# Which engine issues a scan's stores, how often its norm's factors are stored, and where its state is scaled

## The chip, the cores and the metric

The kernel runs on one core of one Trainium2 chip. It uses TensorE (PE in the profile), VectorE (DVE), ScalarE (ACT), GpSimd (POOL), and SyncE (SP), which here issues DMAs and does nothing else. The metric is the time of one execution on the device in microseconds. A time on the chip is the median of a few runs; beside it stands one profiled execution, whose trace every duration below is from.

## The reference

One layer of a decoder: 1024 rows of width 1024, all in f32. A causal block mixes a gated short convolution (A) with a Mamba-2 scan (S) and ends with a gated MLP. Cut to what matters here:

```python
u = rmsnorm(h)
gate_a, gate_s, b_a, c_a, v_a, z, xbc, dt = split(u @ w_in)
A = (b_a * causal_dwconv3(c_a * v_a)) @ w_a_out
xs, B, C = split(silu(causal_dwconv4(xbc) + bias))
# scan: 4 groups of 8 heads of 64, state 128, in chunks of 128 rows
seg = a_cum[l] - a_cum[s]                       # per head, masked causally
y_diag = ((C @ B.T) * exp(seg)) @ (x * dt)
states = B.T @ (x * dt * exp(a_cum[-1] - a_cum))
state  = state * exp(a_cum[-1]) + states        # from chunk to chunk
y = y_diag + (C @ state_before) * exp(a_cum) + d_skip * x
y = y * silu(z)
S = (y * rsqrt(mean(y * y over the group's 512) + eps) * w_norm) @ w_s_out
h = h + (sigmoid(gate_a) * A + sigmoid(gate_s) * S) @ w_o
v = rmsnorm(h)
h = h + (silu(causal_dwconv3(v @ w_1) + b) * (v @ w_3)) @ w_down
out = rmsnorm(h)
```

## The kernel before, in words

**Products.** Activations lie transposed: 128 features on the partitions, rows along the free axis. An f32 product is made of rounded halves: `split` (L148, L149) casts an operand on ScalarE to a high part and takes the rest on VectorE or GpSimd, and `product` (L255) makes 12 matmuls of 128x512 (high by high, high by low, low by high, over four blocks). Two column blocks of a projection are one `Pair`: seven such products on sums and differences of operands and weights (names b11, b21, t1, t2, t3, t4, b22). `load` (L158) brings the weights into three buffers `raw`; seven products use two loads. So while a `Pair` runs, TensorE needs a cast of ScalarE every twelve matmuls, and the names of its waits carry the `Pair`: pt1z is the product with t1 of a pair of z, pt4xb that with t4 of a pair of xBC, pb22cv that with b22 of a pair of c_a and v_a.

**The projections.** First come the gates of group A (`head`), then the list BEFORE and the list BESIDE: xBC (`xbc_pair`, with a convolution of four taps and a Silu in `conv4`), z (`z_pair`, Silu), c_a with v_a (`ca_pair`), b_a (`ba_pair`) and the gates (`gate_pair`, Tanh in `gates_done`). Their results go to DRAM: xBC and z of group g to `xd_[g]`, with ten slots of 128 features for each group (four of x, one of B, one of C, four of z; L545 and L561), b_a's product to `tad` (L586), the gates to `gad` and `gsd` (L596). Before, SyncE issues all of these stores, with those of c_a's branch.

**The scan.** 32 chunks s = 8 g + c (group g of 4, chunk c of 8; a name such as m2_1 is m of group 2, chunk 1) run beside the list BESIDE. `ssd_chunk` is a generator cut into eight parts. A counter `tick` goes up with every product of a `Pair`; chunk s has its due time at 12 + 6 s, and its parts come at fixed distances from it (L53, L54): m's load at -11, the load of `in` at -8, the decay at -6, the transposes at -4, the load of z at -3, the chunk's products at 0, the squares at +3, the norm's factor at +6.

The parts of a chunk, in order:

1. m (L630): the running sums of the decay, one row for each head, from `acd`, sent to all 128 partitions, 128x1024; two buffers.
2. `in` (L633): six slots of `xd_`, 128x6x128; two buffers.
3. The decay, on ScalarE: eight Relu with a bias (L639, one for each head), then one Exp over m (L640).
4. x and B transposed (px L645, pb), C by B (pc L649), x by dt (xd L651, VectorE), x by the decay to the chunk's end (xe L658, eight on ScalarE), d_skip by x (L662, GpSimd), the copy bk of B's transpose (L666, ScalarE, one buffer), C by B masked (L668) and times m (L669).
5. eb (L675), the exp of the running sums, by two loads from `ead`; zt (L680), the four slots of z, one buffer.
6. pd (L687), eight matmuls with m; po (L694), C by the state; pst (L700), B by x. Then y's sum and the state:

```python
        dve.tensor_tensor(xt, xt, tiles(pd), op=ALU.add)          # L701
            dve.tensor_tensor(eb, po, eb, op=ALU.mult)            # L703
            pool.tensor_tensor(xt, xt, tiles(eb), op=ALU.add)     # L704
                pool.tensor_tensor(heads(st), heads(st), ...)     # L711
                dve.tensor_tensor(st, st, pst, op=ALU.add)        # L715
        dve.tensor_tensor(xt, xt, zt, op=ALU.mult)                # L717
        sp.dma_start(yd[g, c // 4][:, :, hts], xt)                # L718
```

7. Squares of y (L721, ScalarE, into eb), two sums on VectorE (L722, L724).
8. pn (L727), a matmul with ones that sums over the partitions; the mean and eps (L729); the power -0.5 (L731, GpSimd) into r, one column of 128 values; r's store into `rd` (L732), half a kilobyte.

x and y stand in the tile of `in` (xt is its first four slots), which is why its rows in the profile are called `in`. y goes to `yd[g, half]`, and y's factors to `rd[g, half]`, each half being four chunks. Both are read again later by `y_half`, for the product with w_s_out.

**After the list** the last chunks run out beside nothing (the loop at L762), and the program goes on with the gated sum of A (`ta_half`, `y_a`), S (`y_half`, `s_out`), w_o, and the MLP. `w_sums` (L779 loads w_down, L770 subtracts, L787 stores the sums to `td`) is given to s_out and y_a as work beside them; its operations need nothing of the mixer.

**What sets the order.** The code is written in the order of the parts, but a scheduler, with a timeline simulation of its own, puts each instruction in its engine's list; each engine then works its list in order. So `w_sums` stands among the last chunks. An instruction that waits holds all that is behind it on its engine, DMA issues included. A DMA takes one of eight completion semaphores in turn over SyncE and ScalarE, and before it issues it waits until the DMA that had the semaphore before has landed. The buffers are rings: m's load of chunk s waits until pd of chunk s - 2 has read m; `in` of chunk s waits until y's store of chunk s - 2 has landed and its squares are done.

The functions touched are `conv4`, `z_pair`, `gates_done` and `ssd_chunk`; `tiny` (L131) gives the small columns.

Of the kernel before, what the change touches and what calls it, by code (L numbers as in the profile page):

```python
# [11 lines left out]
ALU = mybir.AluOpType  # L12
# [3 lines left out]
P = 128  # L16
# [6 lines left out]
HG = NH // NG  # L23
HD = 64
# [3 lines left out]
NCH = SEQ // P  # L28
# [37 lines left out]
def tile_block(  # L66
# [25 lines left out]
    pe, dve, act, pool, sp = nc.tensor, nc.vector, nc.scalar, nc.gpsimd, nc.sync  # L92
# [14 lines left out]
    def big_tile(name, dt=F32, shape=(P, 4, HALF)):  # L107
        return big.tile(list(shape), dt, tag="big", name=name, bufs=NBIG)
# [4 lines left out]
    def b4(name, shape=(P, SEQ)):  # L113
        return cur["b4"].tile(list(shape), F32, tag="b4", name=name, bufs=cur["n"])
# [16 lines left out]
    def tiny(name, w=1):  # L131
        return scr.tile([P, w], F32, tag="tiny", name=name, bufs=12)
# [7 lines left out]
    def const(shape, name, src=None):  # L140
        t = cst.tile(shape, F32, name=name)
        if src is not None:
            sp.dma_start(t, src)
        return t
# [18 lines left out]
    nhalf = const([P, 1], "nhalf")  # L163
# [167 lines left out]
    xd_ = [dram.tile([P, 10, SEQ], F32, name=f"ssd_in{g}") for g in range(NG)]  # L331
# [5 lines left out]
    yd, rd = {}, {}  # L337
# [20 lines left out]
    for t in range(0, NCH, 2):  # L358
        xt = big_tile(f"x{t}", shape=(P, 2, DM))
# [17 lines left out]
    cdb = scm.tile([P, 4, NH, 2], F32, name="cdb")  # L377
# [51 lines left out]
    for j in range(0, 4, 2):  # L429
# [3 lines left out]
        p = Pair(U, w_in[GA + j], w_in[GA + j + 1], f"g{GA + j}", cur["row"])  # L433
        p.first(b4(f"gt{j}"), True)
        head.append(p)
    p = Pair(U, w_in[GA + 4], w_in[GA + 5], f"g{GA + 4}")
# [88 lines left out]
    def ssd_slot(t):  # L525

        return (t // 4, t % 4) if t < 16 else ((t - 16) % 4, 4 + (t - 16) // 4)

    def taps(cv, ci, w, b):

        n = w.shape[1]
        act.activation(  # L532
            cv, ci[:, n - 1 : n - 1 + SEQ], AF.Identity, scale=w[:, n - 1 : n], bias=b
        )
        for j in range(n - 1):
            dve.scalar_tensor_tensor(  # L536
                cv, ci[:, j : j + SEQ], w[:, j : j + 1], cv, op0=ALU.mult, op1=ALU.add
            )

    def conv4(ci, t):  # L540
        cv = b4(f"cv{t}")
        taps(cv, ci, scw[:, t, :], scb[:, t : t + 1])
        act.activation(cv, cv, AF.Silu)
        g, slot = ssd_slot(t)
        sp.dma_start(xd_[g][:, slot, :], cv)  # L545

    def xbc_pair(t):
        cis = [s4(f"xbc{t + i}") for i in range(2)]
# [7 lines left out]
    def z_pair(t):  # L556
        zs = [b4(f"z{t + i}") for i in range(2)]
        pair(U, w_in[ZZ + t], w_in[ZZ + t + 1], f"z{t}", *zs)
        for i, z in enumerate(zs):
            act.activation(z, z, AF.Silu)  # L560
            sp.dma_start(xd_[(t + i) // 4][:, 6 + (t + i) % 4, :], z)  # L561


    taken = {}
# [28 lines left out]
    def gates_done(gts, dst, j):  # L593
        for i, gt in enumerate(gts):
            act.activation(gt, gt, AF.Tanh, scale=0.5)
            sp.dma_start(dst[:, j + i, :], gt)  # L596

    for i, p in enumerate(head):
        if i:
# [9 lines left out]
    def heads(t):  # L609
        return t.rearrange("p (h d) -> p h d", h=HG)  # L610

    def tiles(t):
        return t.rearrange("p (j l) -> p j l", j=4)

    states, stats = {}, {}

    def ssd_chunk(s):

        g, c = divmod(s, NCH)
        nm = f"{g}_{c}"  # L620
        q, cc = c // 2, c % 2
        hsl = slice(g * HG, (g + 1) * HG)
        ts = slice(c * P, (c + 1) * P)
        hts = slice((c % 4) * P, (c % 4 + 1) * P)

        hq = slice(q * NH + g * HG, q * NH + (g + 1) * HG)


        m = ssp.tile([P, HG, P], F32, tag="m", name=f"m{nm}", bufs=2)
        sp.dma_start(m, acd[cc, hq].unsqueeze(0).to_broadcast([P, HG, P]))  # L630
        yield
        inp = ssp.tile([P, 6, P], F32, tag="in", name=f"in{nm}", bufs=2)
        sp.dma_start(inp, xd_[g][:, 0:6, ts])  # L633
        xt, bt, ct = inp[:, 0:4, :], inp[:, 4, :], inp[:, 5, :]
        yield

        for h in range(HG):
            a = tk[:, 0, cc, q, g * HG + h : g * HG + h + 1]
            act.activation(m[:, h, :], m[:, h, :], AF.Relu, bias=a)  # L639
        act.activation(m, m, AF.Exp, scale=-1.0)  # L640
        yield

        px = sd_tile(f"px{nm}")
        for j in range(4):
            pe.transpose(px[:, j * P : (j + 1) * P], xt[:, j, :], ident)  # L645
        pb = sd_tile(f"pb{nm}")[:, :P]
        pe.transpose(pb, bt, ident)
        pc = sd_tile(f"pc{nm}")[:, :P]
        pe.matmul(pc, bt, ct, start=True, stop=True)  # L649
        xd = c2(f"xd{nm}")  # L650
        dve.tensor_tensor(  # L651
            heads(xd), heads(px),
            tk[:, 1, cc, q, hsl].unsqueeze(2).to_broadcast([P, HG, HD]), op=ALU.mult,
        )
        xe = c2(f"xe{nm}")
        for h in range(HG):
            hc = slice(h * HD, (h + 1) * HD)
            act.activation(  # L658
                xe[:, hc], px[:, hc], AF.Copy,
                scale=tk[:, 2, cc, q, g * HG + h : g * HG + h + 1],  # L660
            )
        pool.tensor_tensor(  # L662
            xt, xt, dsk[:, 4 * g : 4 * g + 4].unsqueeze(2).to_broadcast([P, 4, P]), op=ALU.mult,
        )
        bk = ssp.tile([P, P], F32, tag="bk", name=f"bk{nm}", bufs=1)
        act.copy(bk, pb)  # L666
        cb = ssp.tile([P, P], F32, tag="cb", name=f"cb{nm}", bufs=1)
        dve.tensor_tensor(cb, pc, tri, op=ALU.mult)  # L668
        dve.tensor_tensor(m, m, cb.unsqueeze(1).to_broadcast([P, HG, P]), op=ALU.mult)  # L669
        yield  # L670

        eb = c2(f"eb{nm}")
        if c > 0:
            for i in range(2):
                sp.dma_start(  # L675
                    tiles(eb)[i * HD : (i + 1) * HD],
                    ead[cc, hq.start + i : hq.stop : 2].unsqueeze(0).to_broadcast([HD, 4, P]),
                )
        zt = ssp.tile([P, 4, P], F32, tag="z", name=f"zt{nm}", bufs=1)
        sp.dma_start(zt, xd_[g][:, 6:10, ts])  # L680
        yield

        st = states.get(g)
        pd = sd_tile(f"pd{nm}")
        for h in range(HG):
            i, j = h % 2, h // 2
            pe.matmul(  # L687
                pd[i * HD : (i + 1) * HD, j * P : (j + 1) * P],
                xd[:, h * HD : (h + 1) * HD], m[:, h, :], start=True, stop=True,
            )  # L690
        if st is not None:
            po = sd_tile(f"po{nm}")
            for j in range(4):
                pe.matmul(  # L694
                    po[:, j * P : (j + 1) * P], st[:, j * P : (j + 1) * P], ct,
                    start=True, stop=True,
                )
        if c < NCH - 1:
            pst = sd_tile(f"pst{nm}")
            pe.matmul(pst, bk, xe, start=True, stop=True)  # L700
        dve.tensor_tensor(xt, xt, tiles(pd), op=ALU.add)  # L701
        if st is not None:
            dve.tensor_tensor(eb, po, eb, op=ALU.mult)  # L703
            pool.tensor_tensor(xt, xt, tiles(eb), op=ALU.add)  # L704
        if c < NCH - 1:
            if st is None:
                st = ssp.tile([P, HALF], F32, tag="st", name=f"st{g}", bufs=1)
                act.copy(st, pst)
                states[g] = st
            else:  # L710
                pool.tensor_tensor(  # L711
                    heads(st), heads(st),
                    cdb[:, q, hsl, cc : cc + 1].to_broadcast([P, HG, HD]), op=ALU.mult,
                )
                dve.tensor_tensor(st, st, pst, op=ALU.add)  # L715

        dve.tensor_tensor(xt, xt, zt, op=ALU.mult)  # L717
        sp.dma_start(yd[g, c // 4][:, :, hts], xt)  # L718
        yield
        sq = eb  # L720
        act.activation(sq, xt.rearrange("p j l -> p (j l)"), AF.Square)  # L721
        dve.tensor_tensor(sq[:, : 2 * P], sq[:, : 2 * P], sq[:, 2 * P :], op=ALU.add)  # L722
        sums = ssp.tile([P, P], F32, tag="ss", name=f"ss{nm}", bufs=1)
        dve.tensor_tensor(sums, sq[:, :P], sq[:, P : 2 * P], op=ALU.add)  # L724
        yield
        pn = sd_tile(f"pn{nm}")[:, :1]
        pe.matmul(pn, sums, ones[:, :1], start=True, stop=True)  # L727
        rs = tiny(f"yss{nm}")
        dve.tensor_scalar(rs, pn, 1.0 / HALF, EPS, op0=ALU.mult, op1=ALU.add)  # L729
        r = tiny(f"yr{nm}")  # L730
        pool.tensor_tensor(r, rs, nhalf, op=ALU.pow)  # L731
        sp.dma_start(rd[g, c // 4][hts].unsqueeze(1), r)  # L732
        yield

    def at(n, f):
# [261 lines left out]
    for i in range(NFF):  # L997
# [5 lines left out]
        cv = b4(f"fcv{i}")  # L1003
# [221 lines left out]
```

## Time and profile before

| what | value |
|---|---|
| median of 3 runs | 2109.27 us (2107.75 to 2114.36) |
| the profiled execution | 2107.57 us |
| its span in the trace | 2105.9 us |
| mean granted clock of TensorE | 0.967 of full speed |
| DMA, mean over the span | 161 GB/s |

The page's slices (40 of 52.6 us each) show where the engines are full. Each digit is a busy share in tenths, the last row the granted clock:

```profile
PE   6899998997998989897899999997999999999998
DVE  8756986755676557664567562438776677784555
ACT  5354455444744553533333332444433333343444
POOL 7777785674666567566744432347888778853552
PEclk9899998999999999999899999998999999999999
```

Up to about 300 us the projections run without chunks; from there to 930 us the chunks run beside the projections; to about 1070 us the last chunks run with the sums of w_down; the rest is the products with w_a_out, w_s_out and w_o and the MLP. TensorE's row is below 9 mostly in the slices of the chunks (7 to 20). A row of the timeline gives the start in us, the duration, the engine (SPq is SyncE's sequencer), line, operation, out<-in, and in brackets the idle time of the engine before it and what ended it. A row of waits gives who waited for what: total us, times, the longest.

### The profile page before, as it was taken

To read this page: it belongs to the slowest core of one execution; us is meant where nothing else is said; L and a number is where in the kernel's file an instruction comes from. 1 tells how busy PE (TensorE), PEld (TensorE's weight loads), DVE (VectorE), ACT (ScalarE), POOL (GpSimd) and SP (SyncE) were. 2 spreads that over 40 slices of the span, in tenths; PEclk is the share of its full clock that TensorE was granted. 3 is DMA by queue.
4 is the path that set the end of the run, shared out by engine and by line. 5 is a ranking of instruction groups with operands and counts; after the bars stand their busy time and mean duration, and the time that the engine had idled before them with its cause. 6 is when DMAs were issued, how large, how long until landed. Compare 5 with 4: busy or idle time off the path is not lost.

```text
span 2105.9 us, 26136 instructions
## 1 busy us (share of the span) xinstructions
PE 1956.1 (93%) x8978; PEld 1594.3 (76%) x8978; DVE 1365.6 (65%) x1588; ACT 904.3 (43%) x1687; POOL 1306.4 (62%) x959
## 2 busy tenths in 40 slices
PE   6899998997998989897899999997999999999998
PEld 5788877776776777675677888886788888887887
DVE  8756986755676557664567562438776677784555
ACT  5354455444744553533333332444433333343444
POOL 7777785674666567566744432347888778853552
PEclk9899998999999999999899999998999999999999
DMA  4243235545445743667999674442322234468664
GB/s 145 72 157 105 110 131 139 147 119 137 146 119 111 158 142 97 128 165 212 249 282 389 244 248 159 159 161 97 120 105 103 98 130 155 146 210 285 198 200 150
DMA packets 184724, 338.47 MB, mean 161 GB/s; under 512 B 19856, under 2 KB 92304, under 8 KB 183568
## 3 DMA queue, kind: packets, MB, share of 16 engines
q1 hardware_dynamic: 184592, 336.80, 52.0%
q8 instruction: 71, 1.16, 0.3%
q14 instruction: 61, 0.50, 0.1%
HBM read 247.34 MB, written 89.41 MB: 160 GB/s over the span
## 4 chain that ended last, share of the span: by engine, by line
PE 41%; DMA 9%; DVE 2%; POOL 1%; issue 1%; ACT 0%; SPq 0%; POOLq 0%; ACTq 0%; DVEq 0%
PE so L255 7%; DMA td<-wd 3%; PE d L1018 3%; PE d L1020 3%; PE d L1019 3%; PE pt4up L255 3%; PE pb22up L255 3%; PE pt3up L255 3%; PE pt2up L255 3%; PE pb11up L255 3%; PE pt1up L255 3%; PE pb21up L255 3%; PE ya L255 2%; DMA wd<-in_w_down 2%; PE wo L891 1%; PE wo L892 1%
## 5 line engine op out<-in xcount | busy, mean ns | idle before, releaser
L639 ACT ACTIVATE m<-m,tk 128x128 f32<-128x128 f32 x256 | 78.8, 389 | 196.7 <-DMA m<-acd 182.6
L536 DVE SCALAR_TENSOR_TENSOR cv<-xbc,scw,cv 128x1024 f32<-128x1024 f32 x72 | 128.2, 1803 | 18.1 <-ACT cv L532 18.1
L536 DVE SCALAR_TENSOR_TENSOR fcv<-fci,fcw,fcv 128x1024 f32<-128x1024 f32 x44 | 77.8, 1768 | 27.9 <-ACT fcv L532 27.9
L149 POOL TENSOR_TENSOR l_ws<-raw_ws,h_ws 128x512 fp32r<-128x512 f32 x32 | 45.8, 1433 | 78.9 <-issue 29.0
L722 DVE TENSOR_TENSOR eb<-eb 128x256 f32<-128x256 f32 x32 | 21.3, 666 | 83.7 <-ACT eb L721 83.3
L148 ACT CAST h_ws<-raw_ws 128x512 fp32r<-128x512 f32 x64 | 38.5, 621 | 81.5 <-PE so L255 54.7
L255 PE MATMUL so<-yh,h_ws 128*128 128x512 f32 x256 | 69.6, 393 | 1.5 <-ACT h_ws L148 0.7
L658 ACT ACTIVATE xe<-px,tk 128x64 f32<-128x64 f32 x256 | 55.9, 329 | 31.0 <-DVE xd L651 30.9
L255 PE MATMUL so<-yl,h_ws 128*128 128x512 f32 x256 | 68.8, 389 | 0.0
L255 PE MATMUL so<-yh,l_ws 128*128 128x512 f32 x256 | 68.7, 390 | 0.0
L149 DVE TENSOR_TENSOR l_ws<-raw_ws,h_ws 128x512 fp32r<-128x512 f32 x32 | 29.0, 910 | 59.2 <-PE so L255 34.3
L149 POOL TENSOR_TENSOR l_wo<-raw_wo,h_wo 128x512 fp32r<-128x512 f32 x24 | 33.3, 1390 | 52.1 <-ACT h_wo L148 25.0
L292 POOL TENSOR_TENSOR t1up<-raw_2up,raw_1up 128x512 f32<-128x512 f32 x22 | 34.6, 1572 | 46.3 <-DMA raw_2up<-in_w_up 41.8
L715 DVE TENSOR_TENSOR st<-st,pst 128x512 f32<-128x512 f32 x24 | 16.5, 687 | 70.7 <-POOL st L711 63.3
L255 PEld LDWEIGHTS so<-yh,h_ws 128*128 128x128 f32 x256 | 47.4, 188 | 12.8 <-ACT h_ws L148 2.3
L717 DVE TENSOR_TENSOR in<-in,zt 128x512 f32<-128x512 f32 x32 | 44.4, 1388 | 18.7 <-POOL in L704 18.1
L255 PEld LDWEIGHTS so<-yh,l_ws 128*128 128x128 f32 x256 | 48.0, 188 | 10.5 <-DVE l_ws L149 0.5
L255 PEld LDWEIGHTS so<-yl,h_ws 128*128 128x128 f32 x256 | 48.1, 188 | 10.1
L148 ACT CAST h_wo<-raw_wo 128x512 fp32r<-128x512 f32 x48 | 29.7, 622 | 56.7 <-PE wo L892 26.8
L891 PE MATMUL wo<-l_wo,mh 128*128 128x512 f32 x128 | 50.9, 398 | 3.2 <-DVE l_wo L149 3.2
L1006 DVE TENSOR_TENSOR fcv<-fcv,h 128x1024 f32<-128x1024 f32 x22 | 38.9, 1767 | 22.6 <-ACT fcv L1005 22.6
L149 POOL TENSOR_TENSOR l_wa<-raw_wa,h_wa 128x512 fp32r<-128x512 f32 x16 | 27.8, 1743 | 39.3 <-PE ya L255 16.7
(1060 smaller groups left out, 6734.5 us busy)
## 6 DMA issues: line engine op xcount, KB each, us to landing
m<-acd SPq DMA_DIRECT2D x32, 512.0 KB, 5.6
raw_ws<-in_w_s_out SPq DMA_DIRECT2D x32, 512.0 KB, 4.2
ssd_in<-cv SPq DMA_DIRECT2D x24, 512.0 KB, 2.7
in<-ssd_in SPq DMA_DIRECT2D x32, 384.0 KB, 3.8
raw_wo<-in_w_o SPq DMA_DIRECT2D x24, 512.0 KB, 3.4
wd<-in_w_down SPq DMA_DIRECT2D x22, 512.0 KB, 6.2
td<-wd SPq DMA_DIRECT2D x44, 256.0 KB, 5.9
raw_1up<-in_w_up SPq DMA_DIRECT2D x22, 512.0 KB, 3.4
```

The source lines that it names most:

```text
L148: act.copy(hi, v)
L149: (eng or pool).tensor_tensor(lo, v, f32(hi), op=ALU.subtract)
L255: pe.matmul(ps, wt[:, k, :], ct[:, k, :], start=(start and n == 0), stop=(stop and n == 11),)
L536: dve.scalar_tensor_tensor(cv, ci[:, j : j + SEQ], w[:, j : j + 1], cv, op0=ALU.mult, op1=ALU.add)
L639: act.activation(m[:, h, :], m[:, h, :], AF.Relu, bias=a)
L658: act.activation(xe[:, hc], px[:, hc], AF.Copy, scale=tk[:, 2, cc, q, g * HG + h : g * HG + h + 1],)
L717: dve.tensor_tensor(xt, xt, zt, op=ALU.mult)
L891: pe.matmul(pss[t], mh, wl, start=False, stop=False)
L1006: dve.tensor_tensor(cv, cv, h3, op=ALU.mult)
L1018: pe.matmul(ps, aa[0][:, ts], bb[0], start=k == 0, stop=False)
L1019: pe.matmul(ps, aa[0][:, ts], bb[1], start=False, stop=False)
L1020: pe.matmul(ps, aa[1][:, ts], bb[0], start=False, stop=k == KF - 1)
```

## The change

Three things are edited.

- The stores of xBC (24), z (16), the gates (16) and y (32) are issued by ScalarE, and y's store is written behind the squares. The stores of b_a's product, all loads and the factors' stores stay with SyncE.
- The factors of four chunks are columns of one tile of 128x4, and every fourth chunk stores the tile: 8 stores of 512 values each in place of 32 of 128. In DRAM the values lie as before, column c behind column c - 1.
- The scaling of the state by the chunk's decay is written ahead of y's sum.

```diff
 def conv4(ci, t):
-        sp.dma_start(xd_[g][:, slot, :], cv)
+        act.dma_start(xd_[g][:, slot, :], cv)
 def z_pair(t):
-            sp.dma_start(xd_[(t + i) // 4][:, 6 + (t + i) % 4, :], z)
+            act.dma_start(xd_[(t + i) // 4][:, 6 + (t + i) % 4, :], z)
 def gates_done(gts, dst, j):
-            sp.dma_start(dst[:, j + i, :], gt)
+            act.dma_start(dst[:, j + i, :], gt)
 def ssd_chunk(s):
             pe.matmul(pst, bk, xe, start=True, stop=True)
+        if st is not None and c < NCH - 1:
+            pool.tensor_tensor(
+                heads(st), heads(st),
+                cdb[:, q, hsl, cc : cc + 1].to_broadcast([P, HG, HD]), op=ALU.mult,
+            )
         dve.tensor_tensor(xt, xt, tiles(pd), op=ALU.add)
...
             else:
-                pool.tensor_tensor(
-                    heads(st), heads(st),
-                    cdb[:, q, hsl, cc : cc + 1].to_broadcast([P, HG, HD]), op=ALU.mult,
-                )
                 dve.tensor_tensor(st, st, pst, op=ALU.add)
         dve.tensor_tensor(xt, xt, zt, op=ALU.mult)
-        sp.dma_start(yd[g, c // 4][:, :, hts], xt)
         yield
         sq = eb
         act.activation(sq, xt.rearrange("p j l -> p (j l)"), AF.Square)
+        act.dma_start(yd[g, c // 4][:, :, hts], xt)
...
-        r = tiny(f"yr{nm}")
-        pool.tensor_tensor(r, rs, nhalf, op=ALU.pow)
-        sp.dma_start(rd[g, c // 4][hts].unsqueeze(1), r)
+        if c % 4 == 0:
+            stats[g, c // 4] = tiny(f"yr{nm}", 4)
+        r = stats[g, c // 4]
+        pool.tensor_tensor(r[:, c % 4 : c % 4 + 1], rs, nhalf, op=ALU.pow)
+        if c % 4 == 3:
+            sp.dma_start(rd[g, c // 4].rearrange("(c p) -> p c", c=4), r)
```

What the edits make of each engine's list is shown at three places. A row has the line of its own kernel, the operation and out<-in; a number at a name's end is the tile's own and differs between the kernels. In the changed kernel L722 is y's store, L736 the factors' store, L702 the scaling of the state, L709 y's sum (L704 before) and L734 the power (L731 before).

SyncE, where chunks 2_0 to 2_2 begin, before: m2_1 and m2_2 each stand behind a store of factors (rd11), with y's stores and one of xBC (L545) among them.

```order
L675 DMA eb1_7_5614<-ead_109 64x4x128 x2
L586 DMA tad_88<-cc3_5108 128x1024
L732 DMA rd11_100<-yr1_6_5685 128x1
L630 DMA m2_1_5737<-acd_92 128x1024
L158 DMA raw_2xb14_6129<-in_w_in 128x1024
L718 DMA yd11_99<-in1_7_5435 512x1x128
L680 DMA zt2_0_5810<-ssd_in2_86 128x4x128
L633 DMA in2_1_5848<-ssd_in2_86 128x6x128
L158 DMA raw_1z14_6286<-in_w_in 128x1024
L545 DMA ssd_in3_87<-cv12_5813 128x1024
L732 DMA rd11_100<-yr1_7_5897 128x1
L630 DMA m2_2_5942<-acd_92 128x1024
```

The same place in the changed kernel:

```order
L675 DMA eb1_7_5593<-ead_109 64x4x128 x2
L586 DMA tad_88<-cc3_5089 128x1024
L630 DMA m2_1_5713<-acd_92 128x1024
L158 DMA raw_2xb14_6103<-in_w_in 128x1024
L680 DMA zt2_0_5787<-ssd_in2_86 128x4x128
L633 DMA in2_1_5825<-ssd_in2_86 128x6x128
L158 DMA raw_1z14_6261<-in_w_in 128x1024
L736 DMA rd11_100<-yr1_4_5258 128x4x1
L630 DMA m2_2_5917<-acd_92 128x1024
L680 DMA zt2_1_5996<-ssd_in2_86 128x4x128
```

The store ahead of m2_1 is gone, the one ahead of m2_2 is now that of four chunks, and the stores of y and of xBC are no longer in SyncE's list. In the same way m1_3, m3_0 and m3_1 lose the store ahead of them, and m1_2 keeps one.

ScalarE, at the decay of chunk 2_1 and the copy bk of chunk 2_0, before:

```order
L639 ACTIVATE m2_1_5737<-m2_1_5737,tk_225 128x128 x8
L148 CAST h_b11xb14_6054<-raw_1xb14_6051 128x512
L721 ACTIVATE eb1_7_5614<-in1_7_5435 128x512
L148 CAST h_t4z12_5997<-t2z12_5873 128x512
L640 ACTIVATE m2_1_5737<-m2_1_5737 128x1024
L666 COPY bk2_0_5782<-pb2_0_5766 128x128
L532 ACTIVATE cv12_5813<-xbc12_5587,scb_664,scw_662 128x1024
```

And in the changed kernel:

```order
L639 ACTIVATE m2_1_5713<-m2_1_5713,tk_225 128x128 x8
L148 CAST h_b11xb14_6030<-raw_1xb14_6027 128x512
L721 ACTIVATE eb1_7_5593<-in1_7_5416 128x512
L722 DMA yd11_99<-in1_7_5416 512x1x128
L148 CAST h_t4z12_5972<-t2z12_5850 128x512
L640 ACTIVATE m2_1_5713<-m2_1_5713 128x1024
L666 COPY bk2_0_5758<-pb2_0_5742 128x128
L532 ACTIVATE cv12_5790<-xbc12_5565,scb_664,scw_662 128x1024
```

y's store of chunk 1_7 now stands on ScalarE behind the squares, ahead of a cast and of the copy bk; the rest keeps its order.

GpSimd, at y's sum of chunk 2_1, before:

```order
L149 TENSOR_TENSOR l_t4xb14_6234<-t2xb14_6132,h_t4xb14_6233 128x512
L304 TENSOR_TENSOR t3z14_6443<-raw_2z14_6366 128x512
L731 TENSOR_TENSOR yr2_0_6093<-yss2_0_6091,nhalf_80 128x1
L711 TENSOR_TENSOR st2_5912<-st2_5912,cdb_226 128x512
L704 TENSOR_TENSOR in2_1_5848<-in2_1_5848,eb2_1_6017 128x512
```

And in the changed kernel:

```order
L149 TENSOR_TENSOR l_t4xb14_6209<-t2xb14_6106,h_t4xb14_6208 128x512
L304 TENSOR_TENSOR t3z14_6416<-raw_2z14_6338 128x512
L734 TENSOR_TENSOR yr2_0_6069<-yss2_0_6067,nhalf_80 128x1
L702 TENSOR_TENSOR st2_5888<-st2_5888,cdb_226 128x512
L709 TENSOR_TENSOR in2_1_5825<-in2_1_5825,eb2_1_5993 128x512
```

The scheduler had already put the scaling of the state ahead of y's sum, in all 24 chunks that have both, and the two lists are alike here.

## The prediction

> **What bounds the kernel now.** I read the page's table of engines first, then the windows, then the lists of waits of TensorE, ScalarE and SyncE, and then the timeline at the longest waits.
>
> ```profile
> PE 1956.1 (93%) x8978; PEld 1594.3 (76%) x8978; DVE 1365.6 (65%) x1588; ACT 904.3 (43%) x1687; POOL 1306.4 (62%) x959
> ```
>
> TensorE is the bound as a mean. The change touches two stages only, so the windows come next (us, busy time of each engine, granted clock, DMA share, GB/s).
>
> ```profile
> 110.00:300.00 190.00, 188.73 (x846) 155.47 (x845) 143.00 (x129) 89.92 (x140) 147.14 (x105) 1.00 0.34 117
> 300.00:930.00 630.00, 559.55 (x2771) 447.17 (x2770) 410.11 (x528) 312.08 (x733) 396.84 (x310) 0.95 0.52 135
> 930.00:1070.00 140.00, 111.71 (x527) 88.70 (x526) 76.40 (x101) 53.39 (x127) 87.69 (x69) 0.90 0.87 226
> ```
>
> Before 300 us TensorE idles 190 - 188.73 = 1.3 us, though stores of xBC, z and gates already stand on SyncE there: they cost nothing in that stage. From 300 to 930 us the chunks run beside the projections, and TensorE idles 630 - 559.55 = 70.4 us; from 930 to 1070 us, where the sums of w_down join, 28.3 us. The granted clock is 0.95 and 0.90 there and 1.00 where TensorE doesn't idle. So at most about 99 us of idleness, and some lost clock, can be won. TensorE's waits from 300 to 930 us (total, times, longest):
>
> ```profile
> PE pt1xb L255 <- ACT bk L666: 9.8, 1, 9.8
> PE pb22ba L255 <- DVE ba L312: 6.1, 1, 6.1
> PE pt1z L255 <- ACT bk L666: 5.9, 1, 5.9
> PE pb22z L255 <- ACT bk L666: 5.2, 1, 5.2
> PE pb22cv L255 <- ACT bk L666: 4.3, 1, 4.3
> PE pt4xb L255 <- ACT bk L666: 3.6, 1, 3.6
> ```
>
> Six waits make 34.9 of the 70.4 us. One of them, on SyncE, ScalarE and TensorE:
>
> ```profile
> 654.30 0.33 SPq L732 DMA_DIRECT2D rd<-yr  x1
> 654.73 0.37 SPq L630 DMA_DIRECT2D m<-acd  x1
> 667.87 2.44 ACT L639 ACTIVATE m<-m,tk 128x128 f32<-128x128 f32 x8 [16.37 <-DMA m<-acd]
> 673.01 1.22 PE L255 MATMUL pt1z<-us1h,h_t1z 128*128 128x512 f32 x2 [5.89 <-ACT bk L666]
> ```
>
> A store of the norm's factors, then the load of m for chunk 17; m lands 13.1 us after its issue; ScalarE, which runs in order, stands 16.37 us before it; the copy of bk stands behind; TensorE waits 5.89 us. The same pair stands ahead of three more (pt4xb at 532 us, pb22ba at 849, pb22cv at 876):
>
> ```profile
> 517.04 0.32 SPq L732 DMA_DIRECT2D rd<-yr  x1
> 525.53 2.45 ACT L639 ACTIVATE m<-m,tk 128x128 f32<-128x128 f32 x8 [9.42 <-DMA m<-acd]
> 832.55 0.33 SPq L732 DMA_DIRECT2D rd<-yr  x1
> 844.91 2.44 ACT L639 ACTIVATE m<-m,tk 128x128 f32<-128x128 f32 x8 [10.94 <-DMA m<-acd]
> 858.51 0.32 SPq L732 DMA_DIRECT2D rd<-yr  x1
> 871.51 2.44 ACT L639 ACTIVATE m<-m,tk 128x128 f32<-128x128 f32 x8 [10.21 <-DMA m<-acd]
> ```
>
> The other two of the six follow the stores of chunks 0_7 and 1_7 in the same way. From issue to landing (min, median, max), the factors' store first, then m's load:
>
> ```profile
> DMA to landing us min/median/max: 6.8/9.2/12.6
> DMA to landing us min/median/max: 3.7/5.6/13.0
> ```
>
> So the store of half a kilobyte is the slowest DMA of the stage, and what is issued right behind it lands when it does. That, not SyncE's standing still, is what the six waits have in common. SyncE does stand still (whole span):
>
> ```profile
> SPq L545 <- ACT cv L543: 118.6, 20, 12.5
> SPq L718 <- DVE in L717: 105.4, 27, 8.2
> SPq L633 <- DMA yd<-in: 97.6, 22, 9.3
> SPq L732 <- POOL yr L731: 97.5, 26, 9.7
> ```
>
> But m's load goes out as soon as the matmuls of two chunks before have freed its buffer in most chunks, and the loads behind yd wait for yd's landing anyway (third row).
>
> **The change, part by part.** The sum is made against the profiled execution, 2107.6 us (span 2105.9 and 1.7 around it); the median shown is 2109.3, so 1.7 above.
>
> The factors' stores. 32 become 8. Of those in front of a load of m, the order leaves two, in front of m1_2 and m2_2; m1_3, m2_1, m3_0 and m3_1 lose theirs. These four are the waits of 3.6, 5.9, 6.1 and 4.3 us: 19.9 us. What comes in their place is an ordinary chunk. The products with zt count the chunks of 300 to 930 us:
>
> ```profile
> L717 DVE TENSOR_TENSOR in<-in,zt x26: 677/1755/1776, 303.8 to 912.8; 128x512 f32<-128x512 f32 x26
> ```
>
> The 20 chunks without one of the six waits share 70.4 - 34.9 = 35.5 us, 1.8 each; so 19.9 - 4 x 1.8 = 12.7 us are won. From 930 to 1070 us:
>
> ```profile
> PE po L694 <- DVE gt L309: 7.1, 1, 7.1
> PE pc L649 <- DVE gt L312: 5.9, 1, 5.9
> 932.69 0.33 SPq L732 DMA_DIRECT2D rd<-yr  x1
> 933.54 0.42 SPq L779 DMA_DIRECT2D wd<-in_w_down  x1
> 954.03 0.69 DVE L770 TENSOR_TENSOR wd<-wd 128x512 f32<-128x512 f32 x1 [6.22 <-DMA wd<-in_w_down]
> ```
>
> There the same store stands before loads and stores of w_down's sums, on which VectorE stands in order with gt behind. Two waits, 13.0 us, follow stores that go (3_0 and 3_2); less 2 x 1.8 that is 9.4 us. Clock: 0.05 x 630 = 31.5 us are lost beside 70.4 us of idleness, 0.45 for each; I count half of that, 0.2 us for each of the 22.1 us won: 4.4. Together -26.5 us; from -9 (only the later stage's part comes, other waits take over before 930 us) to -40 (all eight waits become ordinary: 34.9 + 13.0 - 8 x 1.8 = 33.5, and 6.7 of clock).
>
> The stores left carry 512 pieces of four bytes in place of 128. No row shows that. The nearest rows (KB, us to landing): half a kilobyte in 128 pieces of 4 bytes, issued with nothing beside it at 401.8 us; one kilobyte in 128 pieces of 8; 64 KB in 128 of 512.
>
> ```profile
> rd<-yr SPq DMA_DIRECT2D x1, 0.5 KB, 6.8
> ced<-ce SPq DMA_DIRECT2D x1, 1.0 KB, 3.8
> acd<-pp SPq DMA_DIRECT2D x2, 64.0 KB, 1.6
> ```
>
> The small pieces cost 6.8 - 1.6 = 5.2 us. If four columns lie beside each other, the store lands in 6.8 as now; if one after the other, in 1.6 + 4 x 5.2 = 22.4. The number of pieces alone isn't the price, for ced has as many and pays 2.2: half the pieces in the same stretch of memory, half the price. The four new columns lie in four separate stretches, so I take 6.8, nothing added, and keep 22.4.
>
> Stores by ScalarE. 32 of y, 24 of xBC, 16 of z, 16 of gates. Duration of an issue (ns, min/median/max):
>
> ```profile
> L718 SPq DMA_DIRECT2D yd<-in x32: 550/552/618, 304.5 to 1077.7; - x32
> L545 SPq DMA_DIRECT2D ssd_in<-cv x24: 319/326/547, 139.7 to 755.3; - x24
> ```
>
> 32 x 0.55 + 56 x 0.33 = 36 us on ScalarE. It is idle half of 300 to 930 us (312 of 630 busy), but the order puts yd's issue between m's Relu and the copy of bk, where TensorE's waits end. I take a quarter, +9; ends 0 (idle time covers them) and 36. SyncE's 118.6 and 105.4 us of waiting go, and I count nothing for that: zt behind yd waits for the same product, in waits for yd's landing, now after the Square too, and the loads of weights for their buffers. What m gains in a few chunks may be 10 us at most; if in came too late, it would cost: it lands well ahead now (1.3 us of TensorE's time in all, next row), and with a Square and an issue (1.2 us) ahead it still does.
>
> ```profile
>   PE px L645: 1.3, 1
> ```
>
> The Trainium skill, page "DMA: Bandwidth & Descriptors", section "Issuing engines are not separate DMA queues", says that issuing from several engines saves only the sequencer's time for the issue. By that rule these stores give SyncE 36 us that it spent beside waiting, and the sum for this part would be 0 or the +9 above; the waits of 118.6 and 105.4 us speak against it as far as something useful stood behind them.
>
> As the program is built, each DMA of SyncE and ScalarE also waits until the one eight places before it, of either engine, has landed. On ScalarE such a wait holds the casts behind it. SyncE issues 863 DMAs in 2106 us by the order, eight in 20 us, more than a landing takes; but from 930 us on a DMA share of 0.87 says that they crowd. Some 16 of the moved stores fall there or beside a slow load, a quarter us each as an estimate: +4, from 0 to 25.
>
> The state's scaling. GpSimd had it ahead of the sum before:
>
> ```profile
> 714.87 1.05 POOL L711 TENSOR_TENSOR st<-st,cdb 128x512 f32<-128x512 f32 x1
> 715.88 1.29 POOL L704 TENSOR_TENSOR in<-in,eb 128x512 f32<-128x512 f32 x1
> ```
>
> The order of GpSimd stays the same there: 0, and this part doesn't do what it says.
>
> Sum: -26.5 + 9 + 4 = -13.5, so 2107.6 - 13.5 = 2094.1 us.
>
> **Rivals.** *The 512 pieces go one after the other* (slower). Each of the 8 stores then holds what is behind it for 22.4 - 6.8 = 15.6 us longer. At 654 us m was 13.0 - 5.6 = 7.4 us late and TensorE waited 5.9, so 1.5 us are covered: the two ahead of m cost 14.1 each; the other six delay zt, in and weights, which have a chunk's time in hand, taken at 3 us: 28.2 + 18 = 46, and 2094 + 46 = 2140. It decides from where the eight cost the 13.5 us that are won: 5.3 us longer each, a landing of 12.1 (2 x 3.8 + 18 x 5.3 / 15.6 = 13.7). For: a store of 4-byte pieces is slow. Against: ced. The skill's same page, section "Specifications", has DMAs under 512 bytes done by reading, modifying and writing; taken piece by piece that is this rival, and ced against rd (3.8 and 6.8 us for 128 pieces each) doesn't bear it out as it stands.
>
> *ScalarE becomes the place of waiting* (about the same): all 36 us of issues count, or the waits for the eighth DMA before cost 25: 2094 + 21 to 27 = 2115 to 2121; with half of it 2105. For: ScalarE is in order, and TensorE's waits end at bk. Against: 50% idle.
>
> *The freed SyncE gives more*: loads of m and weights come early, all eight waits go, and ScalarE's issues cost nothing: 2107.6 - 40 = 2067. Against: m's two buffers and weights' three are not changed.
>
> **How the numbers follow.** Forecast (2080 to 2104): 0.50. More gain (2055 to 2080): 0.12. ScalarE (2104 to 2121): 0.18. Long stores (2121 to 2148): 0.20. A measurement of this kernel tells about 0.3% from no change, 6.3 us: faster is below 2101.3, slower above 2113.9. Faster is the second case and the forecast without its last three us, 0.12 + 0.46 = 0.58; same is the rest of it and most of ScalarE's case, 0.17; slower 0.25. The range 2064 to 2134 leaves out the lower third of the second case and half of the last, 0.14.
>
> **What would show it.** Right: eight stores of factors landing in 7 to 10 us; ScalarE's wait for m before m1_3, m2_1, m3_0 and m3_1 down from 9 to 16 us to some 5, and still long for m1_2 and m2_2; TensorE idle under 55 us from 300 to 930 us. Wrong: those stores land in over 12 us; or ScalarE shows new waits ahead of its DMAs; or TensorE's idle time stays though m lands early.

## The result, and the profile after

The changed kernel takes 2057.32 us (median of 4 runs, 2056.37 to 2058.17) beside 2111.08 us of the kernel before (4 runs). The ratio is 0.9745, with a 95% interval of 0.9727 to 0.9763: 53.8 us, or 2.5%, faster. The forecast was 2094, with a range from 2064; the direction was right, the size was not. The profiled execution has a span of 2055.7 us, 50.2 less than the 2105.9 of before.

The first row of the page of the changed kernel, the table of engines (busy us, share of the span, instructions):

```profile
PE 1935.9 (94%) x8978; PEld 1583.6 (77%) x8978; DVE 1388.2 (68%) x1588; ACT 906.5 (44%) x1687; POOL 1314.1 (64%) x959
```

TensorE did the same 8978 matmuls. Its idle time in the span fell from 2105.9 - 1956.1 = 149.8 to 2055.7 - 1935.9 = 119.8 us, and its busy time fell as well, by 20.2 us. Wall time windows don't compare like with like, since the second kernel is further on at the same time. So here are windows that begin with the first chunk's products (pd of chunk 0_0) and end with the last chunk's (pd of 3_7), of the kernel before and of the changed one (us, length, busy time of each engine, granted clock, DMA share, GB/s):

```profile
297.00:1061.00 764.00, 667.84 (x3282) 532.47 (x3281) 484.04 (x624) 362.65 (x857) 483.43 (x381) 0.94 0.58 149
```

```profile
299.10:1013.50 714.40, 648.92 (x3280) 521.23 (x3279) 499.63 (x621) 362.06 (x855) 489.64 (x377) 0.96 0.53 159
```

49.6 of the 50.2 us are in this stage. TensorE idles 96.2 us in it before (764.00 - 667.84) and 65.5 after, 30.7 less; the same matmuls take 667.84 before and 648.92 after, 18.9 less, and the granted clock goes from 0.94 to 0.96. What remains of TensorE's waits from 300 to 930 us in the changed kernel:

```profile
PE pt1xb L255 <- ACT bk L666: 12.7, 1, 12.7
PE pc L649 <- DVE st L716: 10.9, 6, 4.7
PE pb22z L255 <- ACT bk L666: 7.0, 1, 7.0
```

Of the six waits of the prediction, four are gone. The two that are left follow the two stores of factors that the order keeps in front of a load of m (chunks 1_2 and 2_2); on SyncE and ScalarE, in the changed kernel:

```profile
480.45 0.38 SPq L736 DMA_DIRECT2D rd<-yr  x1
480.94 0.88 SPq L630 DMA_DIRECT2D m<-acd  x1
495.02 2.45 ACT L639 ACTIVATE m<-m,tk 128x128 f32<-128x128 f32 x8 [14.10 <-DMA m<-acd]
665.27 0.36 SPq L736 DMA_DIRECT2D rd<-yr  x1
665.73 0.46 SPq L630 DMA_DIRECT2D m<-acd  x1
679.84 1.57 ACT L639 ACTIVATE m<-m,tk 128x128 f32<-128x128 f32 x5 [15.44 <-DMA m<-acd]
```

They grew, from 9.8 and 5.2 us to 12.7 and 7.0, and m lands 14.1 us after its issue in both. The stores' own time from issue to landing (min, median, max; 6.8/9.2/12.6 for the 32 of before) is now, for eight of four times the pieces:

```profile
DMA to landing us min/median/max: 9.5/11.0/14.0
```

So 32 stores of 9.2 us became 8 of 11.0. And not only m gains. The load of zt (KB, median us to landing), before, in the changed kernel, and in e1, the run below that has the edit of the factors alone:

```profile
zt<-ssd_in SPq DMA_DIRECT2D x32, 256.0 KB, 6.0
```

```profile
zt<-ssd_in SPq DMA_DIRECT2D x32, 256.0 KB, 3.3
```

```profile
zt<-ssd_in SPq DMA_DIRECT2D x32, 256.0 KB, 3.5
```

Why busy time falls is seen in short windows of the kernel before, ahead of the wait of 5.9 us at 667 us and behind it:

```profile
662.00:667.00 5.00, 5.00 (x24) 3.91 (x22) 0.00 (x0) 0.00 (x0) 0.00 (x0) 1.00 0.61 96
673.00:678.00 5.00, 4.99 (x12) 3.92 (x13) 3.97 (x5) 4.98 (x14) 5.00 (x3) 0.50 0.19 57
```

TensorE is full in both, but does 24 matmuls ahead of the wait and 12 behind it: the granted clock is 0.50 for 5 us, so this wait costs 5.9 us of idleness and another 2.5 us of half clock. The trace also keeps the granted clock over time. In the stage of the chunks it is either 1.00 or 0.50; the kernel before has 16 stretches at 0.50, 88.7 us together, and the changed one 9, 51.2 us together. Summed over the time in which TensorE was busy, half clock costs 35.4 us before and 18.2 after, 17.2 less; that is nearly all of the 18.9 us. The Trainium skill, page "TensorE: Matmul & The Clock Gate", section "Part 1: The HAM clock gate (the "warmup" mystery)", says that after an idle window of some 3.4 us the array runs at half rate until it has been busy for about as long again; the 0.50 behind the wait agrees. In this trace waits that the profile gives as 3.0 us have it behind them too (at 596 and 754 us).

### The profile page after: what moved, and what is told of

The parts are those of the page before. It is cut to its first block, busy times and chain, and to the rows that moved or that the text cites. A ratio compares the mean times of both kernels' runs of the same rounds, so it can differ in the third digit from the quotient of the medians.

```text
span 2055.7 us, 26060 instructions
## 1 busy us (share of the span) xinstructions
PE 1935.9 (94%) x8978; PEld 1583.6 (77%) x8978; DVE 1388.2 (68%) x1588; ACT 906.5 (44%) x1687; POOL 1314.1 (64%) x959
## 4 chain that ended last, share of the span: by engine, by line
PE 61%; DMA 11%; DVE 10%; POOL 8%; issue 5%; ACT 4%; SPq 1%; ACTq 0%; POOLq 0%; DVEq 0%
PE so L255 9%; PE ya L255 4%; PE pt2up L255 3%; PE pt3up L255 3%; PE pt4up L255 3%; PE pb11up L255 3%; PE pb22up L255 3%; PE pt1up L255 3%; PE pb21up L255 3%; DMA m<-acd 2%; PE d L1022 2%; PE d L1024 2%; PE d L1023 2%; DVE cv L536 2%; PE wo L895 1%
## 5 line engine op out<-in xcount | busy, mean ns | idle before, releaser
L536 DVE SCALAR_TENSOR_TENSOR cv<-xbc,scw,cv 128x1024 f32<-128x1024 f32 x72 | 132.8, 1867 | 14.3 <-ACT cv L532 14.3
L718 DVE TENSOR_TENSOR in<-in,zt 128x512 f32<-128x512 f32 x32 | 46.5, 1452 | 22.4 <-POOL in L709 19.6
L721 ACT ACTIVATE eb<-in 128x512 f32<-128x512 f32 x32 | 20.3, 634 | 73.5 <-DVE in L718 73.5
```

The lines of the kernel that those rows point to most:

```text
L536: dve.scalar_tensor_tensor(cv, ci[:, j : j + SEQ], w[:, j : j + 1], cv, op0=ALU.mult, op1=ALU.add)
```

## The experiments

The kernels ran in three groups. The time of the kernel before differs a little between groups (2100.2, 2098.0 and 2101.1 us, and 2111.1 with the result), so ratios to it, taken together on one chip, are what is compared.

| run | what it is | median us | ratio to before, 95% interval |
|---|---|---|---|
| e1 | before + factors for four chunks at once | 2042.91 | 0.9727 (0.9697 to 0.9757) |
| e2 | before + all four kinds of stores on ScalarE | 2106.64 | 1.0036 (1.0019 to 1.0053) |
| e3 | before + y's store on ScalarE | 2098.10 | 0.9987 (0.9964 to 1.0009) |
| e4 | before + xBC, z, gates on ScalarE | 2089.91 | 0.9954 (0.9938 to 0.9969) |
| e5 | before + factors as four rows of 512 bytes | 2019.67 | 0.9618 (0.9598 to 0.9638) |
| e6 | before + 32 factors' stores on ScalarE | 2065.88 | 0.9839 (0.9819 to 0.9858) |
| e7 | changed kernel + factors as rows | 2011.71 | 0.9590 (0.9556 to 0.9624) |
| e8 | changed kernel, factors written to be stored last | 2055.20 | 0.9782 (0.9758 to 0.9805) |
| e9 | changed kernel again | 2050.44 | 0.9760 (0.9732 to 0.9787) |
| e10 | e1 + e4 | 2033.54 | 0.9682 (0.9655 to 0.9710) |
| e11 | e5 + e4 | 2018.84 | 0.9612 (0.9585 to 0.9639) |
| e12 | e5 again | 2025.17 | 0.9634 (0.9608 to 0.9660) |

The edit of the state's scaling was not run alone. e2 is the changed kernel without it and without the factors' edit; in its trace VectorE has the same list of 1588 instructions in the same order as in the changed kernel, and in GpSimd's list two of the 959 stand elsewhere, neither of them a scaling. So the edit doesn't change the place of the scaling; that it is worth nothing is argued from this, not timed.

### The parts of the change, one at a time

e1 makes the edit of the factors alone:

```diff
-        r = tiny(f"yr{nm}")
-        pool.tensor_tensor(r, rs, nhalf, op=ALU.pow)
-        sp.dma_start(rd[g, c // 4][hts].unsqueeze(1), r)
+        if c % 4 == 0:
+            stats[g, c // 4] = tiny(f"yr{nm}", 4)
+        r = stats[g, c // 4]
+        pool.tensor_tensor(r[:, c % 4 : c % 4 + 1], rs, nhalf, op=ALU.pow)
+        if c % 4 == 3:
+            sp.dma_start(rd[g, c // 4].rearrange("(c p) -> p c", c=4), r)
```

> The kernel before with one edit: the norm's factors are stored for four chunks at once (8 stores of 512 values). Theory F (the factors' stores hold back the loads of m, and the clock follows TensorE's idleness): nearly all of the 53.8 us is here, 2055 to 2075 us. Theory S (SyncE's standing still at stores was what mattered): here only the four waits of 19.9 us less what comes in their place, 2085 to 2100 us.

e2 makes the edit of the issuing engine alone, for all four kinds of stores (the lines of the change); e3 that of y's store, e4 those of xBC, z and the gates.

> The kernel before with one edit: the stores of xBC, z, gates and y are issued by ScalarE, y's behind the squares; the factors stay 32 stores of SyncE. Theory F: no gain, 2105 to 2122 us (the recorded +13 us of issues and semaphore waits, or nothing). Theory S: most of the gain, 2065 to 2085 us.

> The kernel before with y's store alone issued by ScalarE behind the squares. Theory F: 2105 to 2115 us. Theory S: y's store is the one at which SyncE stood 105.4 us, so a part of the gain, 2080 to 2100 us; the loads of zt then stand for the same product.

> The kernel before with the stores of xBC, z and gates alone issued by ScalarE. Theory F: 2103 to 2113 us. Theory S: the stores of xBC and z, at which SyncE stood 118.6 and 33 us, give the rest of the gain, 2080 to 2100 us.

The factors' edit alone makes the kernel 2.7% faster, at least as much as the whole change. The stores on ScalarE alone make it 0.4% slower; y's alone makes no difference that can be told, and xBC, z and gates alone win 0.5%. The ranges in us were set beside the 2111.1 us of the result, and in this group the kernel before took 10.9 us less. With that taken off them, e2 and e3 lie in the ranges of theory F; e1 came out 1 us below F's, a larger gain than expected, and e4 between the two theories, 1 us above S's. Theory F holds for the factors, theory S falls for the stores taken together: with SyncE freed of all 88 stores of these kinds, but with the 32 factors' stores left, nothing is won. y's store has a price of its own: with xBC, z and gates already on ScalarE it costs 0.8%, from e4's 0.9954 to e2's 1.0036, though e3 shows none for it alone. e1's stage of the chunks, in the same windows as above:

```profile
297.20:1004.50 707.30, 647.73 (x3280) 520.83 (x3279) 499.54 (x624) 362.59 (x857) 496.02 (x380) 0.96 0.53 162
```

Idle 59.6 us against 96.2, busy 20.1 us less. In this run, too, the two waits behind the remaining stores in front of m stand:

```profile
PE pt1xb L255 <- ACT bk L666: 12.4, 1, 12.4
PE pb22z L255 <- ACT bk L666: 8.5, 1, 8.5
```

### What about a store of factors is slow

e5 has TensorE transpose the four columns, so that SyncE stores four pieces of 512 bytes:

```diff
         if c % 4 == 3:
-            sp.dma_start(rd[g, c // 4].rearrange("(c p) -> p c", c=4), r)
+            pr = sd_tile(f"pr{nm}")[:4, :P]
+            pe.transpose(pr, r, ident)
+            rr = sums[:4, :]
+            act.copy(rr, pr)
+            sp.dma_start(rd[g, c // 4].rearrange("(c p) -> c p", c=4), rr)
```

> The kernel before, the factors of four chunks transposed by TensorE to four rows (128x4 to 4x128), copied by ScalarE and stored as four pieces of 512 bytes by SyncE. Theory P (the four-byte pieces hold up what is behind them): the store lands in about 2 us, and the two waits that the stores for four chunks left (12.4 and 8.5 us with them) go too: 2043 less 18 and less some 5 of slow clock, 2012 to 2030 us. Theory N (the number of stores and of SyncE's stops matters, not the pieces): as with eight stores of 512 pieces, 2036 to 2050 us.

The ratio goes from 0.9727 to 0.9618, with intervals that lie apart. There are as many stores and as many bytes as in e1, but no pieces of four bytes. The scheduler moved the stores, and other instructions with them: seven of the eight now stand right in front of a load of m, three in e1. Still m is not held. From issue to landing of m's loads in e5 (min, median, max; at most 13.0 before and 13.8 in e1), for the eight of the 32 loads whose landing this trace has, m1_2 and m2_2 among them (5.3 and 5.9 us):

```profile
DMA to landing us min/median/max: 3.4/5.0/7.0
```

ScalarE's waits for m tell it for all of them (300 to 1070 us; in e1, then in e5):

```profile
ACT m L639 <- DMA m<-acd: 143.8, 25, 14.4
```

```profile
ACT m L639 <- DMA m<-acd: 99.4, 25, 6.3
```

And the stage of the chunks:

```profile
295.00:977.80 682.80, 645.04 (x3290) 519.27 (x3289) 497.66 (x625) 362.73 (x862) 504.00 (x380) 0.98 0.53 167
```

TensorE idles 37.8 us, 58.4 less than before, and is busy 22.8 us less. The transposes are not free: they wait for the power, and behind one of them a product waits for ScalarE's copy, 13.2 of the 37.8 us:

```profile
PE pr L736 <- POOL yr L733: 8.3, 3, 3.6
PE pt4g L255 <- ACT ss L738: 4.9, 1, 4.9
```

The landing of these stores themselves isn't in the trace. That the size of the pieces sets a store's own time, and not their number, is seen in y's store: it has 512 pieces as well, of 512 bytes each, and lands in 2.8 us in e1 at the median, where the 512 pieces of four bytes take 10.4. How much of the 1.1% comes from the other instructions that the scheduler moved isn't separated, and rows stored for each chunk, 32 times, were not run. e7 is the same edit of the changed kernel:

> The changed kernel, its factors stored as four rows of 512 bytes as in the first of these runs. Theory P: the two waits of 12.7 and 7.0 us go, 2028 to 2045 us. Theory N: 2052 to 2062 us.

It came out faster than either theory's range, at 2011.71 us, and its stage of the chunks is the shortest of all:

```profile
297.00:960.40 663.40, 636.68 (x3289) 513.89 (x3288) 506.14 (x621) 362.08 (x861) 499.84 (x379) 0.99 0.52 169
```

Idle is 26.7 us there, the clock 0.99. This kernel is faster than the changed one (0.9745), with intervals that lie apart; against e5 its interval overlaps.

How the pieces hold up what is behind them is in the records of the packets. In the kernel before, for the store at 654.3 us and m's load at 654.7 (start of the packets in us, their size, how many, mean us of one; rows of 664.0 to 664.5 and 665.0 to 667.0 left out):

```
655.0 to 655.5   4 B     144    0.01
655.5 to 656.0   4096 B    6    2.80
656.0 to 656.5   4096 B   10    7.07
658.5 to 664.0   4096 B   24    0.7 to 3.6 (single packets)
664.5 to 665.0   4096 B   10    0.43
667.0 to 667.5   4096 B   49    0.16
```

The small packets, the store's 128 and 16 more of that size, are all taken up within half a microsecond. It is the packets of the next loads that stand: those that start from 655.5 to 656.5 us last up to 8.7 us and end at 658.6 to 665.1, and the store lands at 663.1; later the same size takes 0.16. In e5, behind a store of rows at 653.1 us, they take 0.16 to 0.35 on average over each half microsecond, and 0.9 at most. The Trainium skill, page "DMA: Bandwidth & Descriptors", section "Specifications", says that below 512 bytes a DMA reads, modifies and writes; the runs fit that, as 512-byte pieces are free of the hold, but no record shows the reading.

e6 leaves the 32 stores as they were and has ScalarE issue them:

```diff
-        sp.dma_start(rd[g, c // 4][hts].unsqueeze(1), r)
+        act.dma_start(rd[g, c // 4][hts].unsqueeze(1), r)
```

> The kernel before, its 32 factors' stores unchanged but issued by ScalarE. Theory Q (loads are late because they stand behind the store in SyncE's own queue): the loads of m pass them, 2040 to 2065 us, less what ScalarE's standing at them costs. Theory E (the small pieces occupy what all queues share): m lands as late as before, 2095 to 2115 us.

2065.88 us lies between the two theories, just above the range of Q. Two of m's 32 loads now take over 9 us to land, seven before, and ScalarE's waits for m fall from 182.6 to 59.9 us; in part in their place ScalarE stands for the power that makes the factors, since its DMAs stand in order with the rest (waits of ScalarE, 290 to 1070 us):

```profile
ACT m L639 <- POOL yr L731: 61.0, 6, 12.0
ACT m L639 <- DMA m<-acd: 59.9, 13, 6.9
```

But where a store overlaps a load, the other queue doesn't shield the load: m of chunk 0_3 was issued at 320.9 us, the store at 321.0, and they landed at 330.9 and 331.9; of chunk 3_7 at 974.9 and 975.3, landed at 985.7 and 985.9. In e1, without a store of factors beside them, the same two land after 4.1 and 5.2 us. And zt, which SyncE still loads, takes 5.6 us at the median in e6, against 6.0 before and 3.5 in e1. So neither Q nor E alone: the hold reaches across the queues, as E says, and part of the gain is that the store now comes at another time than m. How much each makes up isn't separated.

e8 keeps the factors of all chunks in one tile and writes the eight stores behind the last chunk:

```diff
-        r = stats[g, c // 4]
...
+        r = rall[:, 8 * g + c : 8 * g + c + 1]
+        pool.tensor_tensor(r, rs, nhalf, op=ALU.pow)
+        if g == NG - 1 and c == NCH - 1:
+            for k in range(NG):
+                for hf in range(2):
+                    sp.dma_start(
+                        rd[k, hf].rearrange("(c p) -> p c", c=4),
+                        rall[:, 8 * k + 4 * hf : 8 * k + 4 * hf + 4],
+                    )
```

> The changed kernel, all eight stores of factors (512 pieces of four bytes) kept back until the last chunk. Theory P: the scan runs as with the rows; eight long stores in a row then stand ahead of loads after the scan, where a DMA share of 0.85 shows: 2035 to 2060 us. Theory N: 2045 to 2060 us; told apart by the waits of ScalarE for m before chunks 1_2 and 2_2, some 5 us by P and 14 by N.

This run didn't do what it was meant to. The scheduler put each store where its columns are ready, so they went out from 392.6 us on, as in the changed kernel (391.3), and ScalarE's longest wait for m was 15.1 us, 15.4 in the changed kernel:

```profile
L737 SPq DMA_DIRECT2D rd<-rall x8: 360/374/1342, 392.6 to 1036.3; - x8
```

The run says nothing on keeping stores back; that is untried.

### What the issuing engine is worth beside fewer stores

Four kernels on one chip, four to six runs each. e10 is e1 with xBC, z and gates on ScalarE and y's store on SyncE; e11 the same with the rows.

> The changed kernel once more, beside the three next runs on one chip, so that what ScalarE's issues cost or win beside the fewer stores can be read from ratios taken together: ratio 0.971 to 0.978. Theory C (ScalarE's issues of y cost, those of xBC, z and gates win a little): slower by 0.2 to 0.8% than the next run. Theory 0 (once the factors' stores are fewer, the issuing engine makes no difference): within 0.2%.

> The kernel before with the factors stored for four chunks at once and the stores of xBC, z and gates issued by ScalarE, y's store left with SyncE. Theory C: the two gains of the parts alone, 2.7% and 0.5%, nearly add up: ratio 0.966 to 0.971. Theory 0: 0.971 to 0.976.

> The kernel before with the factors stored as four rows of 512 bytes and the stores of xBC, z and gates issued by ScalarE, y's store left with SyncE. Theory C: ratio 0.953 to 0.959, the fastest so far. Theory 0: 0.958 to 0.964, as the rows alone.

> The kernel before with the factors stored as four rows of 512 bytes, once more beside the run above: ratio 0.959 to 0.964 by both theories; what tells is the difference from the run above, 0.4 to 0.8% by theory C, under 0.2% by theory 0.

e10 is 0.8% faster than the changed kernel (0.9682 against 0.9760, intervals apart): theory C, for the eight stores of small pieces. The two differ in y's store, and in the state's scaling, which by the lists above changes nothing. In e10 ScalarE carries 56 issues, those that alone won 0.5%; in the changed kernel the 32 of y on top of them lose 17 us. That is the same 0.8% that they cost with 32 stores of factors (e4 and e2). With rows the difference between e11 and e12 is 0.2%, within their intervals, and e7, with y's store on ScalarE, is no slower than e5: there theory 0 holds. Which wait makes the 17 us isn't followed to its end. The lists of waits for the matmul pc (L649) show where they arrive, in e9 and in e10:

```profile
PE pc L649 <- DVE st L716: 9.0, 7, 2.7
PE pc L649 <- DVE gt L312: 8.9, 1, 8.9
```

```profile
PE pc L649 <- DVE st L715: 4.4, 3, 2.6
PE pc L649 <- DVE gt L312: 3.3, 1, 3.3
```

## Why the prediction was right or wrong, point by point

**The factors' stores.** The mechanism was right: the store of small pieces holds m, m holds ScalarE, the copy of bk holds TensorE. m1_3, m2_1, m3_0 and m3_1 lost their long waits, m1_2 and m2_2 kept theirs, as the order had shown. The size, -26.5 us, is the step that failed: e1 alone gives 2.7%, 57 us. Two terms of it were too small. (The parts alone, -57 and e2's +7.5, make -50; the whole change measured -53.8, and -50.7 in e9's group.)

*The waits that go.* I took 22.1 us, from six waits of 3.6 us or more, and gave each an "ordinary" chunk's 1.8 us back. Measured in the stage: 96.2 - 59.6 = 36.6 us, and that although the two waits that stay grew by 5.9. The ordinary chunks were not free of the stores: a store holds whatever is behind it, zt and y's own store (5.6 us at the median before, 2.8 in e1) as well as m. The zt rows above show it. The waits for the state's sum fall, too; which load makes them wasn't followed. From 290 to 1075 us of the kernel before, in e1, and in e5:

```profile
PE pc L649 <- DVE st L715: 10.5, 6, 2.9
```

```profile
PE pc L649 <- DVE st L715: 5.9, 5, 2.4
```

```profile
PE pc L649 <- DVE st L715: 0.3, 1, 0.3
```

In the changed kernel this row is still 10.9 us up to 930 us: with y's store on ScalarE, and stores of small pieces left, this part of the gain doesn't come.

I had priced a transfer where it was seen to stop TensorE for long, not wherever it was in flight.

*The clock.* I took 0.2 us for each us of idleness, half of the 0.45 of the windows, so 4.4 us. Measured: 20.1 us of busy time in e1, 0.55 for each. The halving had no row behind it; the whole 0.45 would have been near. By the record of the clock, e1's stage has 8 stretches at 0.50, 51.2 us together, and half clock costs 17.2 us of busy time there against 35.4 before: 18.2 of the 20.1 us. The loss comes by events, and the stretches behind the six waits alone cost 12.6 us before, nearly three times the 4.4.

**The 512 pieces.** I took 6.8 us to landing, nothing added, from the one store that ran with nothing beside it; the eight take 11.0, 1.8 more than the 9.2 of the small ones. That is neither the 7 to 10 us that were to show me right nor the 12 that were to show me wrong. The rival with 22.4 us fell. That there were fewer of them outweighed that each is longer, but what they still cost is large: e5 takes another 1.1%.

**The issues on ScalarE.** I took +9 and +4 us. Alone, e2 is 0.4% slower, 7.5 us of 2100, over half of that and of the right sign. Its parts differ in sign, which I hadn't seen: xBC, z and gates win 0.5%, and y's on top of them cost 0.8%, 17 us, with 32 stores of factors as with eight. By itself y's costs nothing that can be told, so the parts don't add up, and why is open. The rival in which ScalarE becomes the place of waiting fell as a bound; that in which the freed SyncE gives more had the nearest time, 2067, for a reason that e2 refutes.

**The state's scaling** was put at nothing from the order; no run times it, and the lists of e2 and of the changed kernel agree with that.

**The range** began at 2064, and 2057.3 lies in the lower third of the second case, which it left out. That case went with all eight waits at the price of clock that was too small; with 0.55 per us those 33.5 us alone would have given 52.

## What to carry to other kernels

A DMA's cost is not its bytes: look at the time from issue to landing in the list of DMAs, and where something small lands late, count every load issued behind it, not only the one at which the longest wait shows. If columns must be stored, send them less often, 2.7% here, and turn them into rows first, another 1.1% here after paying for transposes at which TensorE waits 13 us. And price a wait of TensorE by its idle time plus the half clock behind it, as the record of the clock shows it for that wait.

## What the runs showed of the hardware that was not expected

A store of 128 pieces of four bytes, half a kilobyte, made packets of 4096 bytes behind it take up to 8.7 us in place of 0.16, and the hold reached a load issued from the other engine 0.1 to 0.3 us earlier. Four times as many pieces in one store took only 11.0 us at the median, against 9.2. Both are with the traffic of this kernel beside them. Beside e5, which stores rows and a quarter as often, the 32 stores cost this kernel 3.8% of its time, some 80 us for 16 kilobytes.
